# Four elementwise steps of a gated recurrence's heads, from VectorE to GpSimd

## The chip, the cores and the metric

The kernel runs on one core of a Trainium2 chip. The metric is the device time of one launch in microseconds (us), lower is better. A core has five engines that work from queues of their own, each in its order: TensorE (PE in the profile; its weight loads are PEld), VectorE (DVE), ScalarE (ACT), GpSimd (POOL) and SyncE (SP), which issues most of the transfers here.

## What is computed

Two transformer blocks one after the other on 512 tokens of 1024 features. The change touches one part of the first block: a gated recurrence with four heads of 128 keys and 128 values, run forwards and backwards, with queries q, keys k, values v and log decays f.

```python
def hgrn_gates(f_pre, lb):
    log_f = jnp.log(lb + (1 - lb) * jax.nn.sigmoid(f_pre))
    key = (1 - lb) * jax.nn.sigmoid(-f_pre)
...
    def step(state, inp):          # one chunk of one head
        cum = jnp.cumsum(fc, axis=2)
        rel = jnp.where(incl, cum[:, :, :, None, :] - cum[:, :, None, :, :], -jnp.inf)
        scores = jnp.einsum("bhtk,bhsk,bhtsk->bhts", qc, kc, jnp.exp(rel))
        o = (jnp.einsum("bhts,bhsv->bhtv", scores, vc)
             + jnp.einsum("bhtk,bhkv->bhtv", qc * jnp.exp(cum), state))
        new_state = (jnp.exp(last) * state
                     + jnp.einsum("bhsk,bhsv->bhkv", kc * jnp.exp(last - cum), vc))
...
        a = (rms_norm(o_hg, hg_norm_g.reshape(HG_HEADS, HG_DV)) * jax.nn.silu(g_hg)) @ w_branch_a
```

The rest of the program (attention, the branches' products, a router and sixteen experts, then the second block) isn't touched.

## The kernel before

The recurrence is `hgrn`. Keys lie on the 128 partitions and the 512 tokens along the free dimension. `gates(h)` makes one head's inputs by four products of 512 columns with weight blocks of 128 columns (forward gate, backward gate, queries, output gate); each block is loaded as `wraw`, split into a high part `whi` by ScalarE (L88) and a low part `wlo` by VectorE (L90), and multiplied in 24 matmuls (L96 to L98) into a tile `mm`. Then ScalarE takes the sigmoid (L591) and the logarithm (L596), which lie in different tables of functions, so that tables are loaded at L591, L636 and, if the exponentials of L692 come between, at L692. VectorE forms the key K (L595), and the gate's product `gr` (L602).

`hgrn_head` then does the head. VectorE runs two prefix sums over the log decays (scans, L649 and L650), sums the two keys into `KS` (L656) and forms `KL`, the prefix sums less the keys' logarithm (L658). The products of queries and keys are made in seven levels of blocks, from 64 tokens down to 1: for each level VectorE makes the differences `D` (L690, L691), ScalarE their exponential (L692), VectorE the product with q (L693), and TensorE the scores (L666, into `fs` for the two largest levels and the diagonal, into `lv` for the rest). The small levels are put into the tile `C`, under a mask (L701), and in the end C's four diagonal blocks of 32 partitions by 4 times 32 are copied into `P` (L705), which holds the scores of the whole chunk. For the state, ScalarE makes six exponentials (L714, L715), TensorE transposes them (`kt`, L727), ScalarE copies them out (`kn`, L729), TensorE multiplies with the values (`sp`, L732) and VectorE adds up the states `S` (L735). The queries with their decay, `Q`, are an exponential of ScalarE (L720) times q (L737). TensorE gathers P, S and Q into `po` (L741 to L743); the head ends with a norm and the product with `gr` (L749).

Heads run one after the other, and at each `yield` of a head one or more weight products of the next head's `gates` are put in between (for the last head: products for the attention's keys, values and queries, of 256 columns). The order on each engine isn't that of the code: the framework sorts all instructions by priority and by what it takes to be ready, and allots them once, when the program is built. So an operation that is given to another engine can move its neighbours on all engines. At run time each engine follows its own list strictly.

The scratch tiles matter in one place: `KS` and `Q` have one buffer each, `P`, `C`, `R` (which holds K, the prefix sums and the gate) and `gr` two.

Of the kernel before, what the change touches and what calls it, by code (L numbers as in the profile page):

```python
# [14 lines left out]
ALU = mybir.AluOpType  # L15
# [60 lines left out]
class Build:  # L76
# [471 lines left out]
    def hgrn(self):  # L548
        nc, I = self.nc, self.I
        es = ExitStack()  # L550
        hp = self.pool(es, "hgt")
        pp = self.pool(es, "phg", space=PSUM)
        w_in = I["w_in"][0]
        w5 = w_in.rearrange("(k p) (g f) -> p k g f", p=128, f=128)

        def blocks(g0, g1):
            t = self.wp.tile([128, 2, 8, 128], F32, name="wraw", tag="raw", bufs=self.nraw)
            for j, g in enumerate((g0, g1)):
                nc.sync.dma_start(t[:, j], w5[:, :, g])
            for j in range(2):  # L560
                yield self.split(t[:, j], [128, 8, 128])

        self.lev = hp.tile([128, 5, 32], U8, name="lev")
        levf = hp.tile([128, 5, 32], F32, name="levf", tag="KS", bufs=1)
        nc.gpsimd.dma_start(levf, I["k_lev"])
        nc.gpsimd.tensor_copy(self.lev, levf)
        self.seg = hp.tile([128, 512], F32, name="seg")
        nc.gpsimd.memset(self.seg, 1.0)
        nc.gpsimd.memset(self.seg.rearrange("p (b t) -> p b t", t=128)[:, :, 0:1], 0.0)

        def gates(h):

            R = hp.tile([128, 5, 512], F32, name="R", tag="R", bufs=2)
            gr = hp.tile([128, 512], F32, name="gr", tag="gr", bufs=2)
            q = hp.tile([128, 512], F32, name="q", tag="q", bufs=2)
            K, CU, sg = R[:, 0:2], R[:, 2:4], R[:, 4]
            n = 0
            for g0, g1 in ((4 + h, 8 + h), (h, 16 + h)):
                for wh, wl in blocks(g0, g1):
                    ps = self.gemmT(wh, wl, *self.HX, 0, 512)  # L580
                    if n < 2:
                        nc.scalar.activation(R[:, 2 + n], ps, AF.Copy)
                        nc.scalar.activation(R[:, n], ps, AF.Copy, scale=-1.0)
                    elif n == 2:
                        nc.scalar.activation(q, ps, AF.Copy)
                    else:
                        nc.scalar.activation(gr, ps, AF.Copy)
                        nc.vector.tensor_scalar(sg, ps, -40.0, None, op0=ALU.max)
                    n += 1
                    yield  # L590
            nc.scalar.activation(R[:, 0:4], R[:, 0:4], AF.Sigmoid)  # L591
            pre = self.table("natural_log_exp_and_others")

            for d in range(2):
                nc.vector.tensor_scalar(K[:, d], K[:, d], self.oml[:, d, h:h + 1], 1e-38, op0=ALU.mult, op1=ALU.max)  # L595
                self.after(nc.scalar.activation(CU[:, d], CU[:, d], AF.Ln, bias=self.lb[:, d, h:h + 1],  # L596
                                                scale=self.oml[:, d, h:h + 1]), pre)

            self.after(nc.scalar.activation(sg, sg, AF.Exp, scale=-1.0), pre)
            nc.scalar.activation(sg, sg, AF.Ln, bias=self.ones[:, 0:1])  # L600
            nc.scalar.activation(sg, sg, AF.Exp, scale=-1.0)
            nc.vector.tensor_tensor(gr, sg, gr, op=ALU.mult)  # L602
            self.gated_head = q, K, CU, gr
            yield

        def projections():

            for ks in self.wN(w_in, 3072, 256):
                for b in range(4):
                    ps = self.gemmN(ks, *self.HX, b)  # L610
                    nc.scalar.activation(self.KR[:, 2 + b], ps[:, :128], AF.Copy)
                    nc.vector.tensor_copy(self.VN[:, 2 + b], ps[:, 128:])
                    yield
            for n, ks in enumerate(self.wN(w_in, 2560, 512)):
                for b in range(4):
                    ps = self.gemmN(ks, *self.HX, b)
                    nc.scalar.activation(self.QR[:, b, n * 256:(n + 1) * 256], ps, AF.Copy)
                    yield


        for _ in gates(0):
            pass
        for h in range(4):
            fill = gates(h + 1) if h < 3 else projections()
            turns = (0, 2, 4, 6, 9) if h < 3 else (0, 1, 2, 3, 4, 5, 6, 7, 8, 8, 9, 9)
            for i, _ in enumerate(self.hgrn_head(hp, pp, h, *self.gated_head)):
                for _ in range(turns.count(i)):
                    next(fill)
            for _ in fill:
                pass  # L630
        self.nmr = 2
        es.close()
# [11 lines left out]
    def hgrn_head(self, hp, pp, h, q, K, CU, sg):  # L644

        nc = self.nc
        kf, kb, cf, cb = K[:, 0], K[:, 1], CU[:, 0], CU[:, 1]
        v4 = lambda t: t.rearrange("p (b t) -> p b t", t=128)
# [3 lines left out]
        P = hp.tile([128, 512], F32, name="P", tag="P", bufs=2)  # L652
        C = hp.tile([128, 4, 32], F32, name="C", tag="C", bufs=2)
        KS = hp.tile([128, 512], F32, name="KS", tag="KS", bufs=1)
        KL = hp.tile([128, 2, 512], F32, name="KL", tag="KL", bufs=2)
        nc.vector.tensor_tensor(KS, kf, kb, op=ALU.add)  # L656
        nc.scalar.activation(KL, K, AF.Ln)
        nc.vector.tensor_tensor(KL, CU, KL, op=ALU.subtract)  # L658
        lf, lb = KL[:, 0], KL[:, 1]
# [16 lines left out]
        for j in range(4):  # L676
            s = slice(32 * j, 32 * j + 32)
# [24 lines left out]
            yield  # L702
        for j in range(4):
            s = slice(32 * j, 32 * j + 32)
            nc.vector.tensor_copy(v4(P)[s, :, s], C[s])  # L705


        dec = hp.tile([128, 2, 4], F32, name="dec", tag="dec", bufs=2)
# [9 lines left out]
        nc.scalar.activation(S[:, 1, 3], self.S0[:, h, 1], AF.Copy)  # L718
        Q = hp.tile([128, 2, 512], F32, name="Q", tag="Q", bufs=1)
        nc.scalar.activation(Q, CU, AF.Exp)  # L720
        yield
        hv = slice(h * 128, h * 128 + 128)
        for d in range(2):
# [9 lines left out]
            for j, b in enumerate(order):  # L733
                nb = b + 1 if d == 0 else b - 1
                nc.vector.scalar_tensor_tensor(S[:, d, nb], S[:, d, b], dec[:, d, b:b + 1], sp[:, j],  # L735
                                               op0=ALU.mult, op1=ALU.add)
        nc.vector.tensor_tensor(Q, Q, q.unsqueeze(1).to_broadcast([128, 2, 512]), op=ALU.mult)  # L737
        po = pp.tile([128, 512], F32, name="po", tag="po", bufs=2)
        for b in range(4):
            s = slice(b * 128, b * 128 + 128)  # L740
# [1133 lines left out]
```

## Time and profile before

| what | value |
|---|---|
| median of 3 runs | 1756.39 us (1756.29 to 1757.54) |
| the profiled execution | 1756.94 us |
| its span, first to last instruction | 1755.2 us |
| TensorE busy over the span | 1653.5 us (94%) |
| VectorE busy | 813.1 us (46%) |
| ScalarE busy | 650.6 us (37%) |
| GpSimd busy | 125.5 us (7%) |

The four heads of the recurrence lie between about 147 and 306 us of the span. A view by groups of lines gives busy time, mean time of one instruction and the idle time of the engine before it, with what ended that; a timeline gives each instruction's start and duration; a list of waits says which line waited for which. Matmuls overlap, so that the time from one start to the next, and not a row's duration, is what one takes.

### The profile page before, as it was taken

To read this page: it belongs to the slowest core of one execution; us is meant where nothing else is said; L and a number is where in the kernel's file an instruction comes from. 1 tells how busy PE (TensorE), PEld (TensorE's weight loads), DVE (VectorE), ACT (ScalarE), POOL (GpSimd) and SP (SyncE) were. 2 spreads that over 40 slices of the span, in tenths; PEclk is the share of its full clock that TensorE was granted. 3 is DMA by queue.
4 is the path that set the end of the run, shared out by engine and by line. 5 is a ranking of instruction groups with operands and counts; after the bars stand their busy time and mean duration, and the time that the engine had idled before them with its cause. 6 is when DMAs were issued, how large, how long until landed. Compare 5 with 4: busy or idle time off the path is not lost.

```text
span 1755.2 us, 24179 instructions
## 1 busy us (share of the span) xinstructions
PE 1653.5 (94%) x9813; PEld 1157.3 (66%) x9813; DVE 813.1 (46%) x1589; ACT 650.6 (37%) x1152; POOL 125.5 (7%) x161
## 2 busy tenths in 40 slices
PE   5999999999999899999988988899999999999999
PEld 3988779676678743433333324796668988888887
DVE  5536886965443431211211223758774543434342
ACT  4638885666533211001000003456653341414141
POOL 0100000122210000000000000301221000000000
PEclk9999999999999899999999999999999999999999
DMA  9563121212266679999999999342002223232321
GB/s 319 190 192 99 49 74 37 92 37 96 79 198 253 235 300 414 418 419 418 418 419 419 419 420 336 108 148 73 25 25 72 73 96 96 96 96 96 96 96 49
DMA packets 149935, 333.35 MB, mean 190 GB/s; under 512 B 8264, under 2 KB 97072, under 8 KB 130496
## 3 DMA queue, kind: packets, MB, share of 16 engines
q1 hardware_dynamic: 147440, 325.44, 50.2%
q0 software_dynamic: 1632, 5.85, 0.9%
q8 instruction: 77, 1.26, 0.3%
q10 hardware_dynamic: 752, 0.52, 0.1%
q14 instruction: 34, 0.28, 0.0%
HBM read 327.59 MB, written 4.19 MB: 189 GB/s over the span
## 4 chain that ended last, share of the span: by engine, by line
PE 65%; DMA 22%; DVE 6%; ACT 4%; issue 2%; POOL 1%; SPq 0%; POOLq 0%; DVEq 0%; ACTq 0%
PE mm L96 11%; PE mm L97 11%; PE mm L98 11%; DMA mwt<-in_w_exp_gate_dram 4%; DMA mwt<-in_w_exp_up_dram 3%; PE acc L97 3%; PE acc L98 3%; PE acc L96 3%; DMA wraw<-in_w_exp_gate_dram 2%; DMA mwt<-in_w_exp_down_dram 2%; DMA mwh<-in_w_exp_gate_dram 2%; DMA mwh<-in_w_exp_up_dram 2%; PE U L1159 2%; DMA mwh<-in_w_exp_down_dram 2%; PE G L1159 2%
## 5 line engine op out<-in xcount | busy, mean ns | idle before, releaser
L88 ACT ACTIVATE whi<-wraw 128x1024 fp32r<-128x1024 f32 (+1 forms) x171 | 173.4, 1017 | 358.2 <-PE mm L97 179.8
L90 DVE TENSOR_TENSOR wlo<-wraw,whi 128x1024 fp32r<-128x1024 f32 (+1 forms) x171 | 205.4, 1203 | 178.3 <-ACT whi L88 171.8
L96 PE MATMUL mm<-HXl,whi 128*128 128x512 f32 x256 | 104.3, 408 | 0.0
L97 PE MATMUL mm<-HXh,wlo 128*128 128x512 f32 x256 | 102.1, 399 | 1.0 <-DVE wlo L90 1.0
L98 PE MATMUL acc<-whi,uh 128*128 128x512 f32 x256 | 101.3, 396 | 0.0
L97 PE MATMUL acc<-whi,ul 128*128 128x512 f32 x256 | 101.2, 395 | 0.0
L96 PE MATMUL acc<-wlo,uh 128*128 128x512 f32 x256 | 101.2, 395 | 0.0
L98 PE MATMUL mm<-HXh,whi 128*128 128x512 f32 x256 | 101.1, 395 | 0.0
L96 PE MATMUL mm<-H,whi 128*128 128x512 f32 x256 | 99.7, 389 | 0.0
L98 PE MATMUL mm<-H,whi 128*128 128x512 f32 x256 | 99.6, 389 | 0.0
L97 PE MATMUL mm<-H,wlo 128*128 128x512 f32 x256 | 99.6, 389 | 0.0
L1272 DVE TENSOR_TENSOR hy<-hy,U 128x512 f32<-128x512 f32 x16 | 10.3, 683 | 187.5 <-PE U L1159 187.5
L1159 PE MATMUL Y<-mwt,xh 128*64 128x512 f32 x288 | 73.8, 598 | 8.3 <-DVE xh L1275 5.5
L1159 PE MATMUL U<-mwt,xh 128*64 128x512 f32 x256 | 60.3, 597 | 10.9 <-DMA mwt<-in_w_exp_up_dram 10.9
L1826 DVE TENSOR_SCALAR r<-mm 128x512 f32<-128x512 f32 x32 | 22.1, 691 | 85.9 <-PE mm L98 85.9
L1260 ACT ACTIVATE hy<-G 128x1024 f32<-128x1024 f32 x8 | 8.2, 1023 | 132.3 <-PE G L1159 132.3
L97 PEld LDWEIGHTS mm<-HXh,wlo 128*128 128x128 f32 x256 | 48.4, 189 | 13.4 <-issue 2.9
L1159 PE MATMUL G<-mwt,xe 128*64 128x512 f32 x240 | 56.7, 597 | 0.1
L96 PEld LDWEIGHTS mm<-HXl,whi 128*128 128x128 f32 x256 | 48.4, 189 | 11.8 <-issue 2.4
L96 PEld LDWEIGHTS acc<-wlo,uh 128*128 128x128 f32 x256 | 48.1, 188 | 11.6
L97 PEld LDWEIGHTS acc<-whi,ul 128*128 128x128 f32 x256 | 48.1, 188 | 11.6
L98 PEld LDWEIGHTS acc<-whi,uh 128*128 128x128 f32 x256 | 48.1, 188 | 11.6
(555 smaller groups left out, 3863.0 us busy)
## 6 DMA issues: line engine op xcount, KB each, us to landing
mwt<-in_w_exp_up_dram SPq DMA_DIRECT2D x40, 1024.0 KB
mwt<-in_w_exp_gate_dram SPq DMA_DIRECT2D x38, 1024.0 KB
mwt<-in_w_exp_down_dram SPq DMA_DIRECT2D x36, 1024.0 KB
wraw<-in_w_in_dram SPq DMA_DIRECT2D x29, 1024.0 KB
wraw<-in_w_up_dram SPq DMA_DIRECT2D x16, 1024.0 KB
wraw<-in_w_down_dram SPq DMA_DIRECT2D x16, 1024.0 KB
wmt<-in_w_mod_dram SPq DMA_DIRECT2D x12, 1024.0 KB
wraw<-in_w_mod_dram SPq DMA_DIRECT2D x12, 1024.0 KB
```

The source lines that it names most:

```text
L88: i1 = self.nc.scalar.activation(hi, src, AF.Copy)
L90: i2 = self.nc.vector.tensor_tensor(lo, src, hi, op=ALU.subtract)
L96: mm(ps, ah, bl, start=first, stop=False)
L97: mm(ps, al, bh, start=False, stop=False)
L98: mm(ps, ah, bh, start=False, stop=last)
L1159: ins = nc.tensor.matmul(ps[64 * a:64 * a + 64, n], lhs[:, k, 64 * a:64 * a + 64], tl[a][k2][:, n * 512:(n + 1) * 512], start=(k == 0), st ...
L1260: nc.scalar.activation(hs, G, AF.Silu)
L1272: nc.vector.tensor_tensor(hs[:, c], hs[:, c], U[:, n], op=ALU.mult)
L1826: nc.vector.tensor_scalar(r, ps, 0.0, None, op0=ALU.max)
```

## The change

Four steps of each head are given to GpSimd in place of VectorE: the sum of the two keys (KS), the four copies of the diagonal blocks into P, the gate's product (gr), and the product of Q with q. The last is also written further up, right behind Q's exponential. What is computed stays the same.

```diff
-            nc.vector.tensor_tensor(gr, sg, gr, op=ALU.mult)
+            nc.gpsimd.tensor_tensor(gr, sg, gr, op=ALU.mult)
...
-        nc.vector.tensor_tensor(KS, kf, kb, op=ALU.add)
+        nc.gpsimd.tensor_tensor(KS, kf, kb, op=ALU.add)
...
-            nc.vector.tensor_copy(v4(P)[s, :, s], C[s])
+            nc.gpsimd.tensor_copy(v4(P)[s, :, s], C[s])
...
         nc.scalar.activation(Q, CU, AF.Exp)
+        nc.gpsimd.tensor_tensor(Q, Q, q.unsqueeze(1).to_broadcast([128, 2, 512]), op=ALU.mult)
         yield
...
-        nc.vector.tensor_tensor(Q, Q, q.unsqueeze(1).to_broadcast([128, 2, 512]), op=ALU.mult)
```

Since one line is added, lines 721 to 736 of the kernel after stand one further down than before (kt is L728 there, sp L733, S L736). The sorting moves other work too. On GpSimd, which had nothing to do in the recurrence, the kernel after has in the first two heads (KS is the keys' sum, P the score tile, C its diagonal blocks, R holds the keys and the gate):

```order
15 L656 TENSOR_TENSOR KS_1453<-R_1307 128x512
16 L721 TENSOR_TENSOR Q_1778<-Q_1778,q_1309 128x1024
17 L602 TENSOR_TENSOR gr_1308<-R_1307,gr_1308 128x512
18 L656 TENSOR_TENSOR KS_1845<-R_1479 128x512
19 L705 COPY P_1451<-C_1452 32x4x32 x4
20 L602 TENSOR_TENSOR gr_1480<-R_1479,gr_1480 128x512
21 L721 TENSOR_TENSOR Q_2170<-Q_2170,q_1481 128x1024
```

Each of these stands in GpSimd's queue behind the one before it; Q's product of head 0 comes ahead of the gate's.

ScalarE at the end of head 0, before the change (D_1738 is the last level's tile, whi_1877 the first weight block of head 2's gates):

```order
118 L583 ACTIVATE R_1479<-mm_1555 128x512
119 L692 ACTIVATE D_1684<-D_1684 128x1024
120 L591 ACT_TABLE_LOAD
121 L591 ACTIVATE R_1479<-R_1479 128x2048
122 L692 ACT_TABLE_LOAD
123 L692 ACTIVATE D_1738<-D_1738 128x1024
124 L585 ACTIVATE q_1481<-mm_1635 128x512
...
131 L636 ACT_TABLE_LOAD
132 L596 ACTIVATE R_1479<-R_1479,few_126 128x512 x2
133 L657 ACTIVATE KL_1846<-R_1479 128x1024
134 L587 ACTIVATE gr_1480<-mm_1711 128x512
135 L729 ACTIVATE kn_1784<-kt_1780 128x384
136 L88 ACTIVATE whi_1877<-wraw_1874 128x1024
```

and after it:

```order
119 L583 ACTIVATE R_1479<-mm_1555 128x512
120 L88 ACTIVATE whi_1877<-wraw_1874 128x1024
...
125 L692 ACTIVATE D_1738<-D_1738 128x1024
...
128 L591 ACT_TABLE_LOAD
129 L591 ACTIVATE R_1479<-R_1479 128x2048
130 L585 ACTIVATE q_1481<-mm_1635 128x512
131 L636 ACT_TABLE_LOAD
132 L596 ACTIVATE R_1479<-R_1479,few_126 128x512 x2
133 L657 ACTIVATE KL_1846<-R_1479 128x1024
134 L88 ACTIVATE whi_1943<-wraw_1874 128x1024
135 L587 ACTIVATE gr_1480<-mm_1711 128x512
136 L730 ACTIVATE kn_1785<-kt_1781 128x384
```

The last exponential stands ahead of the sigmoid, one table load is gone, and the split of the next block has moved from behind kn to the other side of the sigmoid.

VectorE at the end of head 1, before (wlo_2271 is the low part of the first block of head 3's gates, lv_2135 the scores of the last level):

```order
194 L90 TENSOR_TENSOR wlo_2271<-wraw_2266,whi_2269 128x1024
195 L701 COPY_PREDICATED C_1844<-lev_1300,lv_2058 128x128
196 L701 COPY_PREDICATED C_1844<-lev_1300,lv_2081 128x128
197 L595 TENSOR_SCALAR R_1871<-R_1871,few_126 128x512 x2
198 L656 TENSOR_TENSOR KS_2237<-R_1871 128x512
199 L649 SCALAR_TENSOR_TENSOR R_1871<-seg_1304,R_1871 128x512
200 L650 SCALAR_TENSOR_TENSOR R_1871<-seg_1304,R_1871 128x512
201 L690 TENSOR_TENSOR D_2300<-R_1871 128x2x4x64
202 L658 TENSOR_TENSOR KL_2238<-R_1871,KL_2238 128x1024
203 L588 TENSOR_SCALAR R_1871<-mm_2103 128x512
204 L701 COPY_PREDICATED C_1844<-lev_1300,lv_2135 128x128
```

and after:

```order
188 L701 COPY_PREDICATED C_1844<-lev_1300,lv_2081 128x128
189 L595 TENSOR_SCALAR R_1871<-R_1871,few_126 128x512 x2
190 L649 SCALAR_TENSOR_TENSOR R_1871<-seg_1304,R_1871 128x512
191 L650 SCALAR_TENSOR_TENSOR R_1871<-seg_1304,R_1871 128x512
192 L690 TENSOR_TENSOR D_2300<-R_1871 128x2x4x64
193 L658 TENSOR_TENSOR KL_2238<-R_1871,KL_2238 128x1024
194 L90 TENSOR_TENSOR wlo_2271<-wraw_2266,whi_2269 128x1024
195 L588 TENSOR_SCALAR R_1871<-mm_2103 128x512
196 L701 COPY_PREDICATED C_1844<-lev_1300,lv_2135 128x128
```

The split has moved from ahead of the scans to behind KL. TensorE's list follows: there, between kt and the first po, stood nine matmuls of the next head's first block, and now there are three. At the end of head 2 the split stands in the kernel after as it does here, and a second split follows the last mask.

## Rows read from the trace of the kernel before

**Rows 1.** Busy us (and instructions) of each engine in one head, then granted clock, DMA.

```profile
178.00:216.00 38.00, 35.13 (x384) 27.80 (x382) 32.98 (x55) 32.55 (x51) 0.00 (x0) 0.91 0.19 56
```

**Rows 2.** Timeline of PE between heads 1 and 2: start, us, what.

```profile
215.63 0.55 PE L727 MATMUL kt<-ca,D 128*128 128x128 f32 x3
...
218.96 0.40 PE L97 MATMUL mm<-HXh,wlo 128*128 128x512 f32 x1
219.19 0.40 PE L98 MATMUL mm<-HXh,whi 128*128 128x512 f32 x1
220.39 0.49 PE L741 MATMUL po<-P,V 128*128 128x128 f32 x2 [0.80 <-DVE P L705]
```

**Rows 3.** Who waited for whom, 170 to 262: us in total, times, longest.

```profile
DVE R L649 <- ACT R L596: 8.4, 3, 3.7
...
PE sp L732 <- ACT kn L729: 2.6, 2, 1.5
...
PE po L741 <- DVE P L705: 2.6, 3, 0.9
...
PE mm L96 <- DVE wlo L90: 1.5, 1, 1.5
...
PE mm L97 <- DVE wlo L90: 0.4, 1, 0.4
```

**Rows 4.** Busy us of PE, PEld, DVE, ACT, POOL; the granted clock follows POOL.

```profile
183.00:185.00 2.00, 1.62 (x36) 0.84 (x34) 2.00 (x4) 1.03 (x3) 0.00 (x0) 0.50 0.00 0
...
254.00:256.00 2.00, 0.51 (x12) 0.40 (x3) 2.00 (x5) 1.75 (x6) 0.00 (x0) 0.50 0.01 4
...
219.00:221.00 2.00, 1.20 (x7) 0.67 (x5) 1.93 (x7) 1.97 (x5) 0.00 (x0) 1.00 0.00 0
```

**Rows 5.** The changed lines on DVE: count, ns min/median/max, first and last start.

```profile
L737 DVE TENSOR_TENSOR Q<-Q,q x4: 1214/1218/2486, 169.4 to 279.8; 128x1024 f32<-128x1024 f32 x4
...
L656 DVE TENSOR_TENSOR KS<-R x4: 691/692/692, 147.2 to 242.3; 128x512 f32<-128x512 f32 x4
...
L602 DVE TENSOR_TENSOR gr<-R,gr x4: 676/681/684, 159.5 to 255.7; 128x512 f32<-128x512 f32 x4
...
L705 DVE COPY P<-C x16: 204/218/223, 181.1 to 286.9; 32x128 f32<-32x128 f32 x16
```

**Rows 6.** GpSimd's groups elsewhere in the program: busy us, mean ns, idle before.

```profile
L1559 POOL TENSOR_TENSOR hcv<-hcv,RR 128x512 f32<-128x512 f32 x4 | 5.1, 1284 | 11.2 <-DVE hcv L1557 9.6 <-DVE sm L1728 0.9 <-DVE sm L1727 0.6
...
L1615 POOL TENSOR_TENSOR Xc<-Xc,pc 128x1024 f32<-128x1024 f32 x2 | 4.8, 2422 | 0.1
...
L1731 POOL TENSOR_SCALAR P<-P,sm 128x128 f32<-128x128 f32 x8 | 3.3, 407 | 74.5 <-DVE m L1703 65.3 <-DVE PT L1751 6.4 <-DVE sm L1728 2.8
```

**Rows 7.** Timelines of DVE and POOL where both worked, and POOL alone (374.82).

```profile
519.15 2.29 DVE L90 TENSOR_TENSOR wlo<-wraw,whi 128x1024 fp32r<-128x1024 f32 x1 [0.16 <-ACT whi L88]
...
519.06 1.29 POOL L903 TENSOR_TENSOR M<-M,s 128x512 f32<-128x512 f32 x1 [15.71 <-DVE s L902]
...
377.16 1.85 POOL L851 TENSOR_SCALAR P<-P,sm 128x768 f32<-128x768 f32 x1 [1.43 <-DVE mx L846]
...
374.82 0.91 POOL L851 TENSOR_SCALAR P<-P,sm 128x768 f32<-128x768 f32 x1 [5.69 <-PE mm L98]
```

**Rows 8.** Timelines of ACT, DVE and PE in head 0.

```profile
151.47 1.04 ACT L720 ACTIVATE Q<-R 128x1024 f32<-128x1024 f32 x1
...
151.79 1.22 DVE L658 TENSOR_TENSOR KL<-R,KL 128x1024 f32<-128x1024 f32 x1
...
156.47 1.28 DVE L693 TENSOR_TENSOR D<-D,q 128x512 f32<-128x512 f32 x2
...
157.95 1.07 PE L666 MATMUL fs<-D 128*64 128x64 f32 x48
```

**Rows 9.** ACT's table loads at L692, 140 to 300: count, busy us, mean ns.

```profile
L692 ACT ACT_TABLE_LOAD x2 | 2.6, 1283 | 0.0
```

**Rows 10.** Timeline of DVE between heads 1 and 2.

```profile
216.90 1.22 DVE L658 TENSOR_TENSOR KL<-R,KL 128x1024 f32<-128x1024 f32 x1
```

## The prediction

> **What bounds the kernel now.** I read the windows of the stage first, then the list of who waited for whom, then the timelines of the engines at the places that list names. The gated recurrence runs from about 147 to 306 us. In it no engine has room: in the head from 178 to 216 us TensorE is busy 35.1 of 38 us, VectorE 33.0 and ScalarE 32.6, and GpSimd does nothing [rows 1]. TensorE carries the weight products that are woven into each head; while it is fed it starts one every 0.23 us (218.96, then 219.19) [rows 2], so its time is a floor, and the stage can change by what TensorE waits or runs slowly, and by little else. Its own waits stand in few rows: for P 2.6 us in three waits, for kn 2.6 us in two (the longer 1.5), for a weight split 1.5 us [rows 3]. All of them lie where one head ends and the next begins; I call these places the first, second and third boundary (near 178, 216 and 250 us). After the first and the third the granted clock is 0.50, the lower of the two levels (1.2 GHz), and TensorE had been waiting just before; after the second, with one wait of 0.80 us, it stays at 1.00 [rows 2, 4]. Adding the waits, about 7 us, and some 2 us for each of the two slow stretches, some 11 us (0.6%) is the most that any relief can win here. Head 3 is different: its queries' and keys' products keep TensorE fed, and VectorE waits for it.
>
> **What the change takes off VectorE.** Per head: the product of Q, 1.22 us in the middle (one of the four took 2.49, beside a GpSimd operation); KS 0.69; the gate 0.68; four copies of P, 0.22 each. That is 1.22 + 0.69 + 0.68 + 0.87 = 3.46 us, 13.8 us over four heads [rows 5]. What VectorE gives up is no gain by itself: before the scans it stands idle until ScalarE's logarithm comes, 8.4 us in three waits, the longest 3.7 [rows 3]. KS and the product of Q stood just ahead of the longest, so their 1.9 us there is worth nothing.
>
> **What GpSimd takes for it.** A two-input operation of 128x512 takes it 1.28 us and one of 128x1024 2.42 [rows 6]; so KS, gate and Q cost 1.28 + 1.28 + 2.42 = 5.0 us a head. A 32x128 copy stands in no row: between VectorE's 0.22 [rows 5] and GpSimd's 0.41 for a scaling of 128x128 [rows 6] I take 0.3, so 1.2 for four against 0.90 now.
>
> **The price that decides: the two engines lock each other out.** At 519.06 us GpSimd begins a 128x512 product of 1.29 us; VectorE's weight split, begun 0.09 later, takes 2.29 us in place of 1.22: it lost 1.07, all but 0.22 of the other's run. The other way round, GpSimd's scaling takes 0.91 us alone and 1.85 when it begins behind a split [rows 7]. So each of the 5.0 us on GpSimd can cost VectorE up to 1.07 + 1.07 + (2.42 - 0.22) = 4.3 us a head, against the 3.46 it is spared. Where VectorE would have waited anyway the lock costs nothing; where it is the late engine the lock lands on TensorE.
>
> The Trainium skill (page "SBUF — State Buffer", section "Who interferes with whom") says that the second one to issue fully blocks, and that this holds for a VectorE instruction with two SBUF inputs against any GpSimd instruction that reads SBUF, a copy too, while VectorE instructions with one SBUF input don't contend. The rows above agree for products and scalings; no row has a GpSimd copy against VectorE. By that rule the copies of P have to wait for a split in front of them at the third boundary, and the time is that of the forecast; without it the third boundary, and with it the sum, would come out about 1.1 us lower.
>
> **Term A, head 0.** Q's exponential stands early on ScalarE and ends at 152.5, while VectorE forms KL until 153.0. GpSimd then holds the lock until about 153.0 + 2.2 = 155.2, in a stretch where VectorE runs without a gap and TensorE gets its next scores just in time: the two products D at 156.47 end at 157.75, and fs starts at 157.95 [rows 8]. Everything there moves by 2.2 us. The first half of fs needs only the first of the two, which ends 0.6 earlier; so TensorE stands from 158.0 to about 159.4, and is through with fs some 1.5 late. The gate follows: 1.07 of lock less 0.68 spared, 0.4 more. **A = +1.9**; 0 if the lock doesn't bite.
>
> **Term B, the first boundary.** In the new order ScalarE does the last exponential before the sigmoid, which drops one table load of 1.28 us (there were two such loads in the stage) [rows 9], and splits the next head's weights ahead of the boundary, so four weight products can fill TensorE's wait for kn, and the wait of 0.4 us for wlo goes. Against it: VectorE, and behind it ScalarE's last exponential, come 2 us late out of term A; KL (1.22) now stands before the last mask on VectorE, and so before the copies of P; and the copies take 0.3 longer and may meet a lock. Now TensorE stands 1.5 + 0.9 + 0.4 = 2.8 us; I find 2.2 for kn and 1.5 for P, less the part by which it arrives late itself. **B = 0**, between -2.8 (all waits filled) and +1.5.
>
> **Term C, the second boundary.** Here the order is worse. Before, the next head's weights were split well ahead of VectorE's scans, so nine weight products stood ready between kt and po and TensorE stood only 0.80 us. Now both halves of the split stand behind KL: VectorE's KL ends at 216.90 + 1.22 = 218.1, the split 1.2 later, 219.3, while TensorE is through with kt at 215.63 + 0.55 = 216.2 [rows 2, 10]: a wait of 3.1 us before the first product. P comes about 0.5 us later than TensorE asks for it (KL, split, mask, then four copies). 3.1 + 0.5 - 0.8 = 2.8. Then the lock: Q's product now runs on GpSimd while ScalarE waits for the last pair of D; 2.2 of lock less 1.22 spared there makes the sigmoid, and with it the scans, about 1.0 later. And with 3 us of standing the clock should fall as at the other two boundaries; a product at 0.50 takes twice the 0.23, and some five us of that, half of them waits, cost 1.0. **C = 2.8 + 1.0 + 1.0 = +4.8**, between +1.0 and +7.
>
> **Term D, the third boundary.** Now 1.1 + 0.8 + 1.5 = 3.4 us of standing [rows 3]. The new order is that of the second boundary (split behind KL): 3.1 for the split, then P, whose copies stand behind the last mask while VectorE goes straight into a further split of 1.2 us, which locks them out: 1.6. That is 4.7, or +1.3. On the other hand TensorE arrives some 6 us late, and ScalarE's chain has been able to catch up: at the most all 3.4 are saved. **D = -1.1**, the middle of the two. Head 3 behind it: nothing, since VectorE waits for TensorE there; what moved to GpSimd there only has to be done before the end of the head. Nothing else is moved: SP's queue is the same, and behind 306 us the shift is passed on.
>
> **Sum.** 1.9 + 0 + 4.8 - 1.1 = +5.6 us. The profiled execution took 1756.94 us (its span 1755.2 and 1.7 around it), so 1762.5; the median of the runs, 1756.39, is 0.55 lower, so I forecast 1762.0, slower by 0.32%. A measurement of this kernel can tell about 0.2% (3.5 us) from no change.
>
> **Rivals.** *Given back* (chance 0.30): what makes TensorE late is slack for ScalarE and VectorE, whose chains start again from its products; a delay in one head is then missing from the wait in the next. For it: the boundaries differ in order and not in work. A = 0.4, C = 2.8 without lock and clock, D = -2.5: +0.7, about 1757. *Faster* (0.13): the missing table load and the early split close the first boundary, and the third stands open for less than its 3.4 us because the split there now comes before the mask. This decides if the next head's wlo ends before kt at all three boundaries. -2.8 - 3.4 - 3 for the two slow stretches + 2.8 for the second boundary = -6.4, about 1750. Against it: at the second and third boundary the split stands behind KL in the new order, whatever the durations. *The copies starve* (0.10): each of the four copies of P waits for one VectorE operation of 0.6 to 1.2 us; 3 us more at each of two or three boundaries, on top of the forecast: 1768 to 1771. The forecast itself, 1760 to 1767, has 0.47.
>
> **How the numbers follow.** The range leaves out most of the faster case and the worst of the starved copies, about 0.19 together: 1753.5 to 1768. Faster by over 0.2% (under 1752.9) 0.13; within 0.2% 0.30, the case of the delay given back; slower 0.57, the forecast and the starved copies.
>
> **What would show it.** Right: VectorE operations of 1.8 to 2.5 us and D operations of over 1 us while GpSimd runs; TensorE standing before fs near 158; one row of 2.5 us or more before the first weight product at the second boundary, and a granted clock of 0.50 there; two table loads fewer. Wrong: TensorE's waits at the second boundary under 1.5 us (term C fails), no stretched VectorE rows near 153 (term A and the lock fail), or copies of P far above 0.3 us (the copies starve).

## The result, and the profile after

The kernel after takes 1767.5 us (median of five runs, 1766.1 to 1767.8) against 1757.5 for the kernel before beside it: a ratio of 1.0058, 95% interval 1.0046 to 1.0071. It is slower by 10 us, 0.6%, in the direction and inside the range of the prediction (1753.5 to 1768), though by half a us only, and the sum had 5.6 us. Executions of one kernel also differ by some us near 600 to 640 us, far from the change, with the granted clock there (0.83 in the profiles before and after, 0.69 and 0.66 in those of e2 and e3 below), so the length of the recurrence, from one profile, stands beside each time.

The whole difference arises in the recurrence. I measure its length from the start of ScalarE's first L596 (head 0) to the start of TensorE's last pr (L751): 157.7 us before, 168.4 after, 10.7 more. (In the kernel after the one starts at 147.7 and the other at 316.1; from there to the end of the span both kernels take 1449.6 us.)

Who waited for whom on TensorE in the kernel after, 146 to 316 us (us in total, times, longest), the answer to [rows 3]:

```profile
PE po L741 <- POOL P L705: 4.6, 2, 4.0
PE mm L96 <- DVE wlo L90: 4.2, 2, 3.5
PE sp L733 <- ACT kn L730: 2.5, 1, 2.5
PE mm L97 <- DVE wlo L90: 2.3, 1, 2.3
PE fs L666 <- DVE D L693: 1.5, 1, 1.5
```

That is 15.1 us of standing against 7.1 in [rows 3]: 8 of the 10.7. The rest, 2.7, I put down to the clock. The recurrence in the kernel before, in one window, and a short one behind its first boundary (busy us and instructions of PE, PEld, DVE, ACT, POOL, then the granted clock):

```profile
147.00:306.00 159.00, 151.96 (x1735) 128.23 (x1734) 125.89 (x213) 123.28 (x199) 1.52 (x1) 0.96 0.19 58
...
188.00:190.00 2.00, 2.00 (x9) 1.60 (x9) 2.00 (x5) 0.75 (x1) 0.00 (x0) 0.93 0.00 0
```

and the same window in the kernel after, where TensorE has 84 matmuls fewer by 306 us, and the stretches behind its three boundaries:

```profile
147.00:306.00 159.00, 143.82 (x1651) 119.68 (x1649) 117.75 (x175) 117.33 (x191) 39.05 (x29) 0.94 0.19 58
...
188.00:194.00 6.00, 5.74 (x49) 4.88 (x49) 0.05 (x1) 3.80 (x7) 1.47 (x2) 0.50 0.65 178
224.00:232.00 8.00, 6.89 (x54) 5.54 (x55) 5.96 (x10) 5.00 (x10) 3.17 (x5) 0.59 0.08 18
263.00:266.00 3.00, 2.72 (x13) 2.73 (x13) 2.15 (x4) 1.58 (x2) 1.78 (x4) 0.51 0.00 0
```

The clock is at its lower level (0.50, 1.2 GHz) behind all three, where [rows 4] had it behind two, and behind the first it now lasts beyond 194 us, where it was back at 0.93 from 188 us before. In windows cut closer it is 0.50 from 184.6 to 194.8 us there, against 181.5 to 188.3 before. Each time TensorE had stood just before. TensorE's timeline at the four places of the prediction (start, duration, what, idle before it and what ended that):

```profile
159.23 0.96 PE L666 MATMUL fs<-D 128*64 128x64 f32 x33 [1.46 <-DVE D L693]
...
182.81 0.94 PE L733 MATMUL sp<-V,kn 128*128 128x128 f32 x6 [2.51 <-ACT kn L730]
...
188.26 0.80 PE L741 MATMUL po<-P,V 128*128 128x128 f32 x2 [3.95 <-POOL P L705]
...
224.47 0.50 PE L97 MATMUL mm<-HXh,wlo 128*128 128x512 f32 x1 [2.27 <-DVE wlo L90]
...
227.37 0.80 PE L741 MATMUL po<-P,V 128*128 128x128 f32 x2 [0.63 <-POOL P L705]
...
263.28 0.58 PE L96 MATMUL mm<-wlo,HXh 128*128 128x256 f32 x1 [3.47 <-DVE wlo L90]
```

The longest row is 3.95 us for P at the first boundary. GpSimd's timeline shows why; x4 are the four copies together:

```profile
152.35 2.74 POOL L721 TENSOR_TENSOR Q<-Q,q 128x1024 f32<-128x1024 f32 x1 [4.05 <-ACT Q L720]
160.96 8.88 POOL L602 TENSOR_TENSOR gr<-R,gr 128x512 f32<-128x512 f32 x1 [5.87 <-ACT R L601]
...
184.41 3.79 POOL L705 COPY P<-C 32x128 f32<-32x128 f32 x4 [5.34 <-DVE C L701]
...
225.29 2.02 POOL L705 COPY P<-C 32x128 f32<-32x128 f32 x4 [6.51 <-DVE C L701]
...
296.55 1.27 POOL L705 COPY P<-C 32x128 f32<-32x128 f32 x4 [15.86 <-DVE C L701]
```

At 296.55, with VectorE quiet, four copies take 1.27 us, some 0.3 each, as priced. At the first boundary they take 3.79. VectorE's timeline there, and in head 0 beside Q's product:

```profile
152.75 2.89 DVE L690 TENSOR_TENSOR D<-R 128x512 f32<-128x512 f32 x1
...
184.06 0.29 DVE L701 COPY_PREDICATED C<-lev,lv 128x128 f32<-128x128 uint8 x1
184.25 0.68 DVE L691 TENSOR_TENSOR D<-R,KL 128x512 f32<-128x512 f32 x1
184.85 0.34 DVE L736 SCALAR_TENSOR_TENSOR S<-S,dec,sp 128x128 f32<-128x128 f32 x1
185.11 0.69 DVE L690 TENSOR_TENSOR D<-R 128x512 f32<-128x512 f32 x1
185.71 0.34 DVE L736 SCALAR_TENSOR_TENSOR S<-S,dec,sp 128x128 f32<-128x128 f32 x1
185.97 0.68 DVE L691 TENSOR_TENSOR D<-R,KL 128x512 f32<-128x512 f32 x1
186.57 0.34 DVE L736 SCALAR_TENSOR_TENSOR S<-S,dec,sp 128x128 f32<-128x128 f32 x1
186.83 1.22 DVE L90 TENSOR_TENSOR wlo<-wraw,whi 128x1024 fp32r<-128x1024 f32 x1
```

Behind the last mask (L701) VectorE runs the differences D and the states S in turn, D, S, D, S, D, S, and then the split; each of the first three copies sits through a D and the last one through the split of 1.22 us, and 188.05, the split's end, is 0.2 us before TensorE's po. TensorE stands from 188.26 - 3.95 = 184.31, and the copies begin at 184.41, right behind the mask: at 1.27 us in place of 3.79 they would have left it about 1.4 of the 3.95. None of VectorE's own rows is longer here. In head 0 it is the other way round: Q's product stretches D from 0.68 to 2.89 us.

### The profile page after: what moved, and what is told of

It is laid out like the page before. It is cut to its first block, busy times and chain, and to the rows that moved or that the text cites. A ratio compares the mean times of both kernels' runs of the same rounds, so it can differ in the third digit from the quotient of the medians.

```text
span 1765.7 us, 24196 instructions
## 1 busy us (share of the span) xinstructions
PE 1655.0 (94%) x9813; PEld 1158.5 (66%) x9813; DVE 809.3 (46%) x1561; ACT 648.3 (37%) x1150; POOL 163.9 (9%) x189
## 3 DMA queue, kind: packets, MB, share of 16 engines
q8 instruction: 77, 1.26, 0.3%
## 4 chain that ended last, share of the span: by engine, by line
PE 68%; DMA 17%; DVE 7%; ACT 4%; issue 3%; POOL 1%; SPq 0%; POOLq 0%; DVEq 0%; ACTq 0%
PE mm L96 11%; PE mm L97 11%; PE mm L98 11%; DMA mwt<-in_w_exp_down_dram 5%; PE acc L98 3%; PE acc L97 3%; PE acc L96 3%; PE G L1159 3%; PE U L1159 3%; DMA mwt<-in_w_exp_up_dram 3%; PE Y L1159 3%; DMA wraw<-in_w_exp_gate_dram 2%; DMA mwt<-in_w_exp_gate_dram 2%; PE po L863 2%; PE po L1794 1%
## 5 line engine op out<-in xcount | busy, mean ns | idle before, releaser
L1159 PE MATMUL U<-mwt,xh 128*64 128x512 f32 x256 | 60.3, 596 | 10.2 <-DMA mwt<-in_w_exp_up_dram 10.2
```

Of the source, the lines that this page charges most:

```text
L1159: ins = nc.tensor.matmul(ps[64 * a:64 * a + 64, n], lhs[:, k, 64 * a:64 * a + 64], tl[a][k2][:, n * 512:(n + 1) * 512], start=(k == 0), st ...
```

## The experiments

| kernel | median us | ratio to before, 95% | recurrence, us |
|---|---|---|---|
| before | 1757 to 1757.5 | | 157.7 |
| after | 1767.5 | 1.0058 (1.0046 to 1.0071) | 168.4 |
| e1: Q only filled | 1764.2 | 1.0045 (1.0029 to 1.0061) | 164.3 |
| e2: Q back | 1766.4 | 1.0047 (1.0028 to 1.0065) | 164.8 |
| e3: copies back | 1763.5 | 1.0038 (1.0023 to 1.0054) | 159.3 |
| e4: split written ahead | 1775.8 | 1.0109 (1.0096 to 1.0123) | 171.5 |
| e5: P only filled | 1758.0 | 1.0014 (1.0005 to 1.0023) | 160.9 |
| e6: copies alone | 1764.7 | 1.0049 (1.0035 to 1.0062) | 167.1 |
| e7: Q alone | 1761.1 | 1.0023 (1.0014 to 1.0033) | 161.9 |
| e8: keys' sum and gate alone | 1752.4 | 0.9976 (0.9965 to 0.9988) | 153.3 |
| e9: Q and P only filled | 1752.8 | 0.9980 (0.9964 to 0.9997) | 151.4 |
| e10: gate alone | 1752.9 | 0.9971 (0.9960 to 0.9982) | 153.3 |
| e11: as e8, copies on ScalarE | 1753.0 | 0.9983 (0.9969 to 0.9998) | 154.0 |

The theory after the result: GpSimd's reading and VectorE's two-input operations keep each other waiting; Q's product makes VectorE late, and the copies are themselves late. The rival: the new order of the lists costs the time.

**e1, Q is only written.**

```diff
-        nc.gpsimd.tensor_tensor(Q, Q, q.unsqueeze(1).to_broadcast([128, 2, 512]), op=ALU.mult)
+        nc.gpsimd.memset(Q, 0.5)
```

> The kernel after, with GpSimd filling Q with the constant 0.5 in place of forming the product with q: the queries' decay is left out of the recurrence, nothing else. The lists of all engines stay as they are; GpSimd still writes Q's 128x1024 at the same place but reads nothing. Theory (GpSimd's reading shuts VectorE out, and head 0 and the chains into the scans pay for it): VectorE's D beside it takes 0.7 us instead of 2.89, 2.1, 2.7 and 2.9; the 1.46 us that TensorE stands before fs near 159 us are gone; 1.5 us less from head 0 and 0 to 1.5 from the others, so 1764.5 to 1766, ratio to before 1.0040 to 1.0049. Rival (the new order alone costs the time): 1767.5, 1.0058, and the wait before fs stays. Second rival (writing shuts VectorE out as well): D stays over 1.5 us and the time within 0.5 us of 1767.5.

VectorE's timeline in head 0 has the D that was stretched back at its length:

```profile
152.97 0.68 DVE L690 TENSOR_TENSOR D<-R 128x512 f32<-128x512 f32 x1
```

GpSimd's fill of 128x1024 begins at 152.6 and takes 0.95 us beside it, and no wait before fs is left. The recurrence is 4.1 us shorter with the same lists, the time 3.3 (the intervals of the two ratios overlap): it is the reading that shuts VectorE out, and a fill doesn't. The waits for wlo also shrink, from 2.3 and 3.5 to 1.3 and 1.8 us, so part of what term C and D put down to the order was Q's delay. But P's waits at the second and third boundary grow, to 1.7 and 3.4 us: the copies, asked for earlier, wait there too.

**e2, Q's product back on VectorE.** The line is moved back to its old place as `nc.vector.tensor_tensor`.

> The kernel after, with Q's product alone given back to VectorE at its old line; TensorE's and ScalarE's lists stay those of the kernel after, on VectorE the product (1.22 us in the kernel before) stands right behind the D products of the last level. Theory (lock): head 0 wins its 1.46 us before fs back, as VectorE's D is no longer stretched by 2.2 us and the 1.22 us fit into its wait for ScalarE; the other heads 0 to 1: 1765 to 1766, ratio 1.0043 to 1.0049. Rival (order): TensorE's and ScalarE's lists are the same, so 1767.5, 1.0058. If VectorE had no room for it: over 1767.5.

Recurrence 3.6 us shorter, the same within half a us as e1: VectorE had room for its 1.22 us, and Q's product on GpSimd costs about 4 us here. The time, 1766.4, is above what was expected, and its interval, which overlaps that of the kernel after, is too wide to say more.

**e3, the copies back on VectorE.**

```diff
-            nc.gpsimd.tensor_copy(v4(P)[s, :, s], C[s])
+            nc.vector.tensor_copy(v4(P)[s, :, s], C[s])
```

> The kernel after, with the four copies of the diagonal blocks given back to VectorE. Theory (copies that wait their turn behind VectorE's two-input operations): TensorE's 3.95 us before po at the first boundary fall to under 1.5, those at the second (0.63) to about 0.3; 3 us less, 1763.5 to 1765.5, ratio 1.0035 to 1.0046. The lists of TensorE, VectorE and ScalarE change too (more weight products stand ahead of po, and the split of the next weights moves at all boundaries), so another 1.5 us either way may come from that. Rival (the last mask is late, not the copies): the wait for P at the first boundary stays over 3 us and the time at 1767 or more.

TensorE's two largest waits in e3:

```profile
PE sp L733 <- ACT kn L730: 6.4, 3, 2.6
PE po L741 <- DVE P L705: 1.9, 2, 1.1
```

The waits for P fall to 1.9 us and no matmul waits for wlo; the recurrence is 9.1 us shorter. Its twelve times spread from 1756.3 to 1767.1, so their median tells less than the trace. The lists moved as well, so this alone doesn't price the copies.

**e4, the next head's first split written ahead of the head.** An extra `yield` ahead of the first block's product lets the loop draw the split of the next head's gates first; the lists differ from those of the kernel after from the second boundary on, where head 3's gates begin.

```diff
                 for wh, wl in blocks(g0, g1):
+                    if n == 0: yield
                     ps = self.gemmT(wh, wl, *self.HX, 0, 512)
...
             fill = gates(h + 1) if h < 3 else projections()
+            if h < 3: next(fill)
```

> The kernel after, with the first weight split of head 3's gates written ahead of the head before it begins: on ScalarE it then stands ahead of KL's logarithm and on VectorE ahead of KL at the second boundary; the first boundary and head 0 keep their lists. Theory (term C: the place of the split costs): TensorE's 2.3 us for wlo near 224 us fall under 0.7, and with them the stretch at half clock behind it: 2 to 3.5 us less, 1764 to 1765.5, ratio 1.0037 to 1.0046. Rival (given back): P becomes what TensorE waits for there, at 2 us or more, and the time stays within 1 us of 1767.5, 1.0052 to 1.0064.

Theory and rival both missed the time. The rival's mechanism is what the rows show: P grows to 1.46 us at the second boundary, where the rival had 2 or more, and to 3.86 at the third. TensorE's timeline at the second and third boundary:

```profile
224.19 0.50 PE L97 MATMUL mm<-HXh,wlo 128*128 128x512 f32 x1 [1.95 <-DVE wlo L90]
...
228.92 0.80 PE L741 MATMUL po<-P,V 128*128 128x128 f32 x2 [1.46 <-POOL P L705]
...
262.71 1.35 PE L733 MATMUL sp<-V,kn 128*128 128x128 f32 x6 [1.84 <-ACT kn L730]
...
268.56 0.79 PE L741 MATMUL po<-P,V 128*128 128x128 f32 x2 [3.86 <-POOL P L705]
```

The wait for wlo lost 0.3 us, since the split came ahead of KL and still behind the scans; KL went back by as much as the split came forward (1.1 us each, against the scans). At the third boundary the wait for wlo is gone, and P (3.86) and kn (1.84) took its place. The recurrence grew by 3.1 us. The timed runs are 8 us over the kernel after; the profiled one took 1771.6, so 4 us of that aren't in this trace and stay open.

**e5, P's blocks are only written.**

```diff
-            nc.gpsimd.tensor_copy(v4(P)[s, :, s], C[s])
+            self.after(nc.gpsimd.memset(v4(P)[s, :, s], 0.5), last)
```

(`last` is the head's last masked copy; the line sets the order of the lists and no wait.)

> The kernel after, with GpSimd filling the four diagonal blocks of P with 0.5 in place of copying them from C (the diagonal blocks' scores are left out of the output); VectorE's and ScalarE's lists stay those of the kernel after, on TensorE one group of three weight products moves behind the first po. The fills read nothing and wait for no mask, so P is never late. Theory (the copies themselves are late, each behind a two-input operation of VectorE): TensorE's waits for P (4.6 us) go, and the end of the recurrence (pr of the last head, 10.5 us later in the kernel after than before) comes 4 to 5 us earlier: 1762 to 1764, ratio 1.0026 to 1.0037. Rival (something else is as late as P, the next weights' split or kn): these waits grow instead, and the time stays over 1765.5.

TensorE's waits in e5:

```profile
PE mm L96 <- DVE wlo L90: 4.3, 2, 3.6
PE sp L733 <- ACT kn L730: 2.6, 1, 2.6
PE mm L97 <- DVE wlo L90: 2.3, 1, 2.3
PE fs L666 <- DVE D L693: 1.5, 1, 1.5
```

The four largest are those of the kernel after, to 0.1 us; P's 4.6 are gone and 1.4 in three small ones are new. The recurrence is 7.5 us shorter: 3.2 of waits, and the rest goes with the clock (0.98 over 147 to 306 in place of 0.94). The time is 4 us under what the theory had. The fills wait for no mask and run at 179.3 us, 5 us ahead of the copies' place and not beside that row of VectorE's; so this shows what it is worth that P is never late, which is more than the copies' stretching (some 2.5 of the 3.95 us at the first boundary).

**e6, the copies alone.** The kernel before with `nc.gpsimd.tensor_copy` at L705.

> The kernel before, with the four copies of the diagonal blocks alone given to GpSimd. Theory: GpSimd's copies wait their turn in VectorE's row of two-input operations at each of the three boundaries; copies of 0.6 us and more beside VectorE's, TensorE's waits for P (2.6 us in three before) come to 6 us or more, the end of the recurrence 4 to 8 us later: 1761 to 1765, ratio 1.0023 to 1.0046. Rival (the copies are late only in the company of the other three parts): waits for P of 3 to 4 us, 1757.5 to 1759, ratio under 1.0012.

TensorE's two waits in e6, and after them the copies' line:

```profile
PE po L741 <- POOL P L705: 10.4, 3, 4.0
PE sp L732 <- ACT kn L729: 2.9, 3, 1.5
...
L705 POOL COPY P<-C x16: 279/556/1358, 180.9 to 296.7; 32x128 f32<-32x128 f32 x16
```

In the kernel before this one step, four copies of 32x128 a head, costs 7.7 us of time, 9.4 of the recurrence: three waits of 2.9, 3.5 and 4.0 us where [rows 3] has 2.6 together. The four copies take 3.23, 3.20 and 3.54 us together at the three boundaries and 1.27 in the last head. Up to the first po the lists are those of the kernel before without the copies, and there the wait for P goes from 0.95 to 2.91; behind it the lists of all three engines move too, so the rest of the price isn't the copies' alone. Nothing of Q or the gate is in this kernel, so the copies starve by themselves.

**e7, Q's product alone.** The kernel before with the product moved up and given to GpSimd.

> The kernel before, with the product of Q and q alone given to GpSimd, early; ScalarE's list stays that of before, TensorE's moves a few weight products. Theory (lock, term A): VectorE's D beside it takes 2 to 3 us in place of 0.7, TensorE stands 1.5 us before fs near 158; the other heads 0 to 2: 1758.5 to 1760.5, ratio 1.0009 to 1.0020. Rival (no wait of its own without the other parts): within 1 us of the kernel before.

VectorE's timeline in head 0:

```profile
155.51 2.89 DVE L690 TENSOR_TENSOR D<-R 128x512 f32<-128x512 f32 x1
```

TensorE stands 1.4 us before fs, as term A has it, and 6.0 us for kn in three waits; the recurrence is 4.2 us longer, 4.0 in time, more than the 1.5 to 3.5 that were expected. The delay is not all in head 0: in every head one VectorE operation is stretched, to 2.9 or 3.2 us, and kn comes late at each boundary.

**e8, keys' sum and gate alone.** The kernel after with both lines of e2 and e3 back.

> The kernel after with Q's product and the copies both back on VectorE at their old lines: only the keys' sum and the gate's product are on GpSimd. Theory (the copies and Q's product are the cost): within 2 us of the kernel before, ratio 0.9990 to 1.0012, although most of the lists' new order is kept. Rival (the new order, which the gate's move brings, costs): 1761 or more, ratio over 1.0023.

It beats both kernels, 5 us under the kernel before, which neither theory nor rival had. TensorE's four largest waits:

```profile
PE sp L732 <- ACT kn L729: 1.8, 1, 1.8
PE po L741 <- DVE P L705: 1.4, 2, 1.1
PE mm L96 <- DVE wlo L90: 0.4, 1, 0.4
PE fs L666 <- DVE D L693: 0.4, 1, 0.4
```

With those of 0.3 and less they make 4.5 us, in place of 7.1, and the clock is 0.99 over 147 to 306. The gate of head 0 takes 8.87 us on GpSimd here too, and nobody waits for it.

**e9, both fills.** The edits of e1 and e5 together: the order of the kernel after without the reading of Q and of the copies.

> The kernel after, with GpSimd filling Q and the diagonal blocks of P with 0.5 in place of the product and the copies (the queries' decay and the diagonal blocks' scores are left out); the lists of TensorE, VectorE and ScalarE are those of the kernel after but for one group of three weight products. What remains of the change is the new order, with the keys' sum and the gate on GpSimd. Theory (the reading of Q's product and of the copies is the whole cost): 3 us under the kernel with the fills of P alone, the end of the recurrence at 303 to 306 us (305.6 before): 1753 to 1757.5, ratio 0.998 to 1.0004; the waits for wlo behind the scans shrink to 1.3 and 1.8 us, as where Q alone was filled. Rival (the new order costs 3 us or more by itself, as term C had it): 1760 or more, ratio over 1.0015, with waits for wlo over 2 us at the second and third boundary.

TensorE's three largest waits in e9:

```profile
PE sp L733 <- ACT kn L730: 1.8, 1, 1.8
PE mm L96 <- DVE wlo L90: 1.7, 1, 1.7
PE mm L97 <- DVE wlo L90: 1.2, 1, 1.2
```

The same order, and the recurrence is 17 us shorter than in the kernel after, 6.3 shorter than before. The rival falls: with this order the time is under that of the kernel before, although TensorE waits 2.9 us for wlo. What the order costs by itself isn't told apart, since the fills also free P of the mask (P's waits were 2.6 us in [rows 3]) and VectorE of its part of the work. Taken singly from here, Q's product costs 9.5 us (e5) and the copies with their wait for the mask 12.9 (e1); together they cost 17, so in part they wait at the same time.

**e10, the gate alone.** The kernel before with `nc.gpsimd.tensor_tensor` at L602.

> The kernel before, with the gate's product alone given to GpSimd. TensorE's and ScalarE's lists are those of the kernel with keys' sum and gate on GpSimd (2 table loads fewer than before), VectorE keeps the sum. Theory (that kernel's gain of 4 us comes from the new lists, and the sum is worth nothing since it stood ahead of a wait): the same time, 1751.5 to 1753.5, ratio 0.9970 to 0.9982. Rival (the sum on GpSimd takes part in the gain): 1754.5 to 1757, ratio 0.9986 to 1.0.

The same as e8 within the intervals: the keys' sum is worth nothing on either engine, as the prediction had it. The recurrence's window in e10:

```profile
147.00:306.00 159.00, 153.00 (x1754) 128.05 (x1752) 129.29 (x212) 122.63 (x200) 14.85 (x5) 1.00 0.21 62
```

The clock never falls in it, and two of ScalarE's table loads (1.28 us each, [rows 9]) are gone. Whether the gain is the new order's or that of the 0.68 us taken off VectorE in each head was not separated.

**e11, the copies on ScalarE.** As e8, with `nc.scalar.activation(v4(P)[s, :, s], C[s], AF.Copy)` at L705.

> Keys' sum and gate on GpSimd, Q's product on VectorE, and the four copies of the diagonal blocks on ScalarE. Theory (only GpSimd's copies wait for VectorE's two-input operations): copies of some 0.2 us each on ScalarE beside VectorE's, waits for P of 1.5 us at most, and a time within 3 us of 1752.5, ratio 0.996 to 0.9995; the lists of all engines are another time new. Rival (any engine that copies beside VectorE is held up): copies of over 0.5 us, waits for P of 3 us, 1758 or more, ratio over 1.0005.

The copies in e11:

```profile
L705 ACT ACTIVATE P<-C x16: 292/308/309, 183.5 to 284.2; 32x128 f32<-32x128 f32 x16
```

None is stretched (0.29 to 0.31 us, a little over the 0.2 expected), and no matmul waits for P (TensorE's weight loads do, 1.4 us in three waits). So it isn't copying beside VectorE that is slow, but GpSimd's copying. The time is that of e8 and e10.

## Why the prediction was right in sign and short in size

**Term A** held: 1.46 us before fs against 1.5, D at 2.89, the lock as described. Its last part, 0.4 for the gate, didn't show as a wait: the gate itself was held up (8.88 us), nobody waited for it, and VectorE lost 0.91 at its end (the product of 1.59 us shown at the end of this text). What the term missed is the rest of Q's price: e1, e2 and e7 put it at 3.6 to 4.2 us, where A and C's lock together had 2.9.

**Term B is the step that failed.** It had 2.2 for kn and 1.5 for P, less TensorE's own lateness, 0 in all. kn took 2.51, near enough; P took 3.95, and nothing was given back for the lateness. The sentence at fault is "the copies take 0.3 longer and may meet a lock": it named the lock and gave it no price. The four copies took 3.79 us in place of 1.2; at 1.27 they would have left P about 1.4 late, near the 1.5, and the other 2.5 is the lock. The place gained 3.6 us of standing over the 2.9 of [rows 3], and the half clock behind it lasted 3.4 us longer (10.2 against 6.8). The rival of the starving copies had the mechanism and the price, 3 us a boundary, at a chance of 0.10: in the kernel after it shows in full at one boundary (at the others the four take 2.0 and 2.2 us, and TensorE, late from the split, waits 0.6 for them and not at all), and in e6 at all three. The rows for a better chance were there: the copies stand behind the last mask, where VectorE has D products and a split to run, and [rows 7] has GpSimd's scaling at 1.85 us behind a split.

**Term C** came near in size and was half wrong in cause. Predicted standing 3.1 and 0.5, seen 2.3 and 0.6, and the clock fell as said (0.59 for 8 us), at more than the 1.0 it was priced at: 0.41 of 8 us is 3.3 us of full clock, by estimate, less what TensorE stood in them. But the order's share is 1.2 us (e9) and Q's about 1.0 (2.3 against 1.3 in e1), which is the lock term's size; and e4 shows that mending the order hands the wait on to P.

**Term D** missed: 3.5 us stand against 3.3, so +0.2 and not -1.1; the lateness of TensorE bought nothing, as VectorE was late too. The 1.6 for P was not seen: the first copy took 1.20 us beside the split, as said, but all four were done at 266.28, while TensorE, which had its split at 263.28, worked until 266.4 at the half clock on what stood ahead of po. **Head 3** had a wait of 0.76 us for wlo where I had nothing.

So the sum came nearer than its terms. It had A 1.9, B 0, C 4.8 and D -1.1; the standing added is A 1.5, B 3.6, C 2.1, D 0.2 and head 3 0.8, and some 2.7 go with the clock. What was missed in B, D, head 3 and the clock (3.6, 1.3, 0.8 and 1.7) is in part made up by what was too much in C and A (1.7 and 0.4). The range held by half a us, which is luck: 1767.5 lies just over the 1760 to 1767 of the forecast, and one of the signs of being wrong, copies far above 0.3 us, is there (0.67 to 1.36 at the first boundary), while a row of 2.5 us at the second boundary is not (2.27). "Faster" was the fate of the same order without the reading (e9), and of the gate alone (e8, e10), near the 1750 that the rival named.

## What to carry to other kernels

Before giving GpSimd a small read of SBUF, look at what VectorE has queued at that moment: the price of a copy is not its own 0.3 us but the two-input operations that it sits through, one for each copy, and four copies in a row pay four times. Give it what nobody waits for soon (the gate, 8.9 us and free), and leave to VectorE or ScalarE what TensorE asks for next. A change of four parts is worth splitting: here the gate gained 4 to 5 us, and the copies and Q's product lost 15 together (e8 against the kernel after).

## What the runs showed of the hardware

The gate's product on GpSimd, 1.26 to 1.28 us alone, took 8.86 to 8.88 us in head 0 of every kernel that had it there. In the kernel after it begins at 160.96; VectorE then issues ten two-input operations without a gap, each at its usual 0.68 or 1.21 us, and the gate ends at 169.84, 1.24 us after the mask L701 begins, with the product behind that mask stretched. VectorE's timeline:

```profile
168.60 0.29 DVE L701 COPY_PREDICATED C<-lev,lv 128x128 f32<-128x128 uint8 x1
168.80 1.59 DVE L693 TENSOR_TENSOR D<-D,q 128x512 f32<-128x512 f32 x1
```

The copies, too, got in while VectorE ran an operation that reads PSUM (L736), and in e6 two of them took 0.28 us each beside L588, which reads PSUM alone, and the next two 1.19 and 1.36 beside KL and the split. But Q's product, 2.40 us before its end at 155.09, got in between KL and D, with no such operation between; what lets GpSimd in there is open. The Trainium skill (page "SBUF — State Buffer", section "Who interferes with whom") has it that a VectorE instruction with two SBUF inputs doesn't contend with a GpSimd instruction which only writes; the fills of Q in e1 and e9 agree (0.95 and 0.96 us for 128x1024, D at 0.68 beside it). Its exemption of VectorE instructions with one SBUF input, which the prediction gives, holds by the page only outside their two-port modes; no term rests on it. The same section has the order of issue decide who blocks; the gate, issued ahead of ten VectorE operations that all went before it, does not agree.
